# A hybrid decoder layer in split fp32: the high and low parts of its matmul operands placed 32 bytes apart modulo 512

## The chip, the cores and the metric

The kernel runs on one core of one Trainium2 chip. The metric is the device time of one execution in microseconds, the median over several runs. Durations of single instructions come from one profiled execution.

## The reference

One layer of a decoder, batch 1, 256 tokens, model width 2048, all float32. Cut to what matters:

```
proj = h @ w_in                      # 2048 x 6144: q, k, v of 8 differential and 8 MoBA heads of 128
a_out = diff_attention(q_d, k_d, v_d, lam, ...)   # two softmaxes a head, a norm over the head
b_out = moba_attention(q_m, k_m, v_m, ...)        # at 256 tokens: causal softmax attention
mix = concat(a_out, b_out) @ w_out   # 2048 x 2048
h = layer_norm(ALPHA * h + mix)
u = h @ w_up                         # 2048 x 11264: gate and value, 5632 columns each
f = (silu(causal_conv3(gate)) * value) @ w_down   # 5632 x 2048
out = layer_norm(ALPHA * h + f)
```

## The kernel before

**Split products.** Every large matmul is worked out in float32r with both operands cut in two: hi is the operand rounded (a ScalarE copy, lines 129, 799, 990, 1019), lo is the operand minus hi (a VectorE subtraction, lines 130, 809, 1003, 1023; for some, a ScalarE copy with the sign changed and an accumulating DMA from GpSimd's queue, lines 797 and 807). A product is the sum of hi by hi, hi by lo and lo by hi, all accumulated in one PSUM bank. The weights stream from HBM into raw tiles (four of 2048 columns), and from there into six tiles hl of 2 x 1024 columns, hi first and lo right behind it.

**Two forms of product.** In the feature form (`mm_feature`, line 206, for q and k, and `up_half`, line 829, for the up projection) the weights are the stationary operand and the activations stream. The activations lie as [hi of 256 tokens, lo of 256 tokens] for each block of 128 features, in the tiles x2 (xa, xb) and later h2 (ha, hb) in the same place. A block takes two matmuls: wh with all 512 columns, then wl with the 256 columns of hi. In the token form the activations are stationary and 512 columns of weights stream, three matmuls: (hi, wh), (hi, wl), (lo, wh). So work the v projection (stationary x2), the out projection (stationary mh and ml, `mm_token`, line 220, two banks at a time), the down projection (stationary aparts or pparts) and the tail (stationary tails). `mm_first` (line 561) does one block of the up projection in the token form with 256 columns.

Every matmul loads its own stationary operand; TensorE does this (PEld in the profile) beside the matmul before it.

**The down projection** is done in pairs of 128-feature blocks, by seven products instead of eight on sums and differences of activations and weights (`unit_weights`, `product`); the weight sums' parts are in bparts (in the place of z), one and hl. The last pairs of the second half are done plainly (`plain_weights`, `plain_product`), the last four blocks at the end (`split_tail`, `mm_tail`).

**Order.** The first stage (v, q, k, attention, out projection, first norm) is written out by hand, with attention's steps hung between weight tiles by `at`. From the third tile of the up projection on, a planner (`order`) simulates each engine with a cost for each task and sorts the tasks; groups of four down products are set between tiles of the up projection. Rings (`raw_ring`, `hl_ring`, `b_ring`, ...) tell it when buffers come free.

**Places in memory.** Tile pools are laid out one behind another in each partition, in the order in which they are opened: keep, raws, splits, small, then first and work in the first stage, zone and duo in their place afterwards. All large tiles are multiples of 512 bytes long. keep begins with the tile shift, of 32 bytes, which nothing uses; then come x2 (h2 later, tag t2), back (480 bytes) and z, so that x2 and h2 start 32 bytes above the other tiles, modulo 512, and z and all pools behind it start where they would without both. mh, ml and val are in first.

Of the kernel before, what the change touches and what calls it, by code (L numbers as in the profile page):

```python
# [16 lines left out]
P = 128  # L17
D = 2048
# [32 lines left out]
def hymba_layer(ctx: ExitStack, tc: tile.TileContext, a: dict):  # L51
# [18 lines left out]

    bank = [psum.tile([P, 512], F32, name=f"bank{i}") for i in range(8)]


    loaded, parts = {}, {}

# [39 lines left out]
    def split(i, half, both=None):  # L115

        if i >= NS or (i, half) in parts:
            return
        t = loaded[i] if half == 0 else loaded.pop(i)
        if both is None:  # L120
            both = splits.tile([P, 2, 1024], F32R, name="hl")
            hi, lo = both[:, 0], both[:, 1]
        else:
            hi, lo = both[:, half], both[:, 2 + half]
        for x, y in pieces(i, half):
            if i < 4 and x % 512 == 0:
                split_x(4 * i + x // 512, 4 * i + (y + 511) // 512)
            s = slice(x - 1024 * half, y - 1024 * half)
            ACT.activation(hi[:, s], t[:, x:y], AF.Copy)  # L129
            DVE.tensor_tensor(lo[:, s], t[:, x:y], hi[:, s].bitcast(F32), ALU.subtract)  # L130
        parts[i, half] = (hi, lo)
# [381 lines left out]
    for i in range(first_o, last[0]):  # L513
        begin(i)
        if i == last[0] - 1:
            both = first.tile([P, 4, 1024], F32R, name="both", tag="big")
# [268 lines left out]
    def split_up(n, x, by_dma):  # L785
# [1 line left out]
        deps = [load_task[n]] if n in load_task else []  # L787

        def alloc():
            both = splits.tile([P, 2, 1024], F32R, name="hl")  # L790
            hl_of[n, x] = both[:, 0], both[:, 1]

        def first():
            alloc()
# [135 lines left out]
    part_ring = Ring(2)  # L930
    part_of, part_use, part_done = {}, {}, {}

    def pair_parts(q, h):
        def high():
            t = part_of[q, h] = duo.tile([P, 2, 7 * P], F32R, name="aparts")
            ACT.activation(t[:, 0], acts[q].rearrange("p a b -> p (a b)"), AF.Copy)

        def low():
            t = part_of[q, h]
            DVE.tensor_tensor(t[:, 1], acts[q].rearrange("p a b -> p (a b)"), t[:, 0].bitcast(F32), ALU.subtract)  # L940
# [21 lines left out]
    def unit_weights(q, h):  # L962
# [24 lines left out]
        s_use += [t1, t2, t3, t4]  # L987

        def high_a():
            ACT.activation(U()["a"][:, 0], U()["raw"][:, 0:1024], AF.Copy)  # L990

        def new_a():
            U()["a"] = splits.tile([P, 2, 1024], F32R, name="hl")
            if apart:
                ACT.activation(U()["a"][:, 1], U()["raw"][:, 0:1024], AF.Copy, scale=-1.0)
            else:
                high_a()

        def low_a():
            if apart:  # L1000
                POOL.dma_start(U()["a"][:, 1], U()["raw"][:, 0:1024], accum_op=ALU.add)
            else:
                DVE.tensor_tensor(U()["a"][:, 1], U()["raw"][:, 0:1024], U()["a"][:, 0].bitcast(F32), ALU.subtract)

        def high_1():
            U()["1"] = zone.tile([P, 2, 512], F32R, name="one")
            ACT.activation(U()["1"][:, 0], raw("11"), AF.Copy)

        def low_1():
            DVE.tensor_tensor(U()["1"][:, 1], raw("11"), U()["1"][:, 0].bitcast(F32), ALU.subtract)  # L1010

        def high_b(j):
            if apart:
                t = splits.tile([P, 2, 1024], F32R, name="hl")
                U()["b", j] = t.rearrange("p j (c w) -> p j c w", c=2)
# [3 lines left out]
            ACT.activation(U()["b", j][:, 0], U()["T"][:, 2 * j:2 * j + 2], AF.Copy)  # L1019

        def low_b(j):
            b = U()["b", j]
            DVE.tensor_tensor(b[:, 1], U()["T"][:, 2 * j:2 * j + 2], b[:, 0].bitcast(F32), ALU.subtract)  # L1023

        ha = act(1024, new_a, [load])
        a_use = hl_ring.use(ha)
# [31 lines left out]
    def product(q, h, m, first, last):  # L1058
# [1 line left out]
        s = SLOT[left] * P  # L1060

        def fn():
            al = part_of[q, h][:, :, s:s + P]
            u = unit[q, h]
            if where == "a":
                wh, wl = (u["a"][:, j, 512 * c:512 * (c + 1)] for j in range(2))
            elif where == "1":
                wh, wl = u["1"][:, 0], u["1"][:, 1]
            else:
                wh, wl = (u["b", int(where[1])][:, j, c] for j in range(2))  # L1070
            dst = bank[m - 1]
            mm(dst, al[:, 0], wh, first, False)
            mm(dst, al[:, 0], wl, False, False)
            mm(dst, al[:, 1], wh, False, last)

        d = unit_done[q, h]
        deps = part_done[q, h] + d[where]
# [6 lines left out]
    def plain_parts(q):  # L1084
# [1 line left out]
            DVE.tensor_tensor(acts[q][:, 3], acts[q][:, 2], acts[q][:, 3], ALU.subtract)  # L1086

        def high():
            t = part_of[q, 1] = duo.tile([P, 2, 4 * P], F32R, name="pparts", tag="aparts")
            ACT.activation(t[:, 0], acts[q][:, 0:4].rearrange("p a b -> p (a b)"), AF.Copy)  # L1090

        def low():
            t = part_of[q, 1]
            DVE.tensor_tensor(t[:, 1], acts[q][:, 0:4].rearrange("p a b -> p (a b)"), t[:, 0].bitcast(F32), ALU.subtract)

        k = dve(P, back, act_use[q][2:])
        t0 = act(4 * P, high, [k])
# [6 lines left out]
    def plain_weights(q):  # L1104
# [3 lines left out]
        for j in range(2):  # L1108
            s = slice(1024 * j, 1024 * (j + 1))

            def high(j=j, s=s):
                U()[j] = splits.tile([P, 2, 1024], F32R, name="hl")
                ACT.activation(U()[j][:, 0], U()["raw"][:, s], AF.Copy)

            def low(j=j, s=s):
                DVE.tensor_tensor(U()[j][:, 1], U()["raw"][:, s], U()[j][:, 0].bitcast(F32), ALU.subtract)

            t = act(1024, high, [load])
            use = hl_ring.use(t)
# [6 lines left out]
    def plain_product(q, m):  # L1126
# [4 lines left out]
        stop = b == 7 and q == N_PAIRS - 1 and j == 1  # L1131

        def fn():
            al = part_of[q, 1][:, :, s:s + P]
            wh, wl = (unit[q, 1][j][:, x, 512 * c:512 * (c + 1)] for x in range(2))
            mm(bank[b], al[:, 0], wh, start, False)
            mm(bank[b], al[:, 0], wl, False, False)
            mm(bank[b], al[:, 1], wh, False, stop)
# [161 lines left out]
    def split_tail(i, x, by_dma):  # L1300
# [3 lines left out]
        def alloc():  # L1304
            if early:
                if i == 0:
                    tail_hl["first"] = keep.tile([P, 2, 2, 1024], F32R, name="first", tag="z")
                both = tail_hl["first"][:, i]
            else:
                both = splits.tile([P, 2, 1024], F32R, name="hl")  # L1310
            tail_hl[i, x] = both[:, 0], both[:, 1]

        def high(first):
            if first:
# [26 lines left out]

    def split_acts():
        def high(i):
            aps[i] = zone.tile([P, 2, S], F32R, name="tails", tag="act", bufs=9)
            ACT.activation(aps[i][:, 0], act_slot(2 * N_PAIRS + i).rearrange("p a b -> p (a b)"), AF.Copy)

        def low(i):
            src = act_slot(2 * N_PAIRS + i).rearrange("p a b -> p (a b)")
            DVE.tensor_tensor(aps[i][:, 1], src, aps[i][:, 0].bitcast(F32), ALU.subtract)

        for i in range(4):
            t = act(S, lambda i=i: high(i), [act_done[2 * N_PAIRS + i]])
# [8 lines left out]
    def mm_tail(dst, t, c, start, o=0, w=512):  # L1361
        ts = slice(t * P, (t + 1) * P)
        for i in range(4):
            x = c % 2 * 512 + o
            wh, wl = (y[:, x:x + w] for y in tail_hl[i, c // 2])
            ah, al = (aps[i][:, j, ts] for j in range(2))
# [204 lines left out]
```

## Time and profile before

| | |
|---|---|
| median of 3 runs | 1118.74 us (1117.76 to 1122.53) |
| the profiled execution | 1117.88 us, of which the span of instructions 1116.1 us |
| TensorE busy | 1100.2 us, 5878 matmuls |
| VectorE busy | 916.6 us |
| ScalarE busy | 702.3 us |
| GpSimd busy | 75.9 us |
| mean granted TensorE clock | 0.997 |
| DMA | 249.89 MB, 224 GB/s |

How to read the profile: PE is TensorE's matmuls and PEld its weight loads, DVE is VectorE, ACT ScalarE, POOL GpSimd, SP the queue that issues most DMAs. A group's line gives the code line, engine and operation, the tiles as output<-inputs, sizes, count, then busy time in us, the mean of one in ns, and the idle time before. All split matmuls have one line, 204 (the helper `mm`), so they are told apart by their tiles: bank<-moving,stationary. Matmuls are pipelined: the mean of one is longer than the time from the start of one to the start of the next.

### The profile page before, as it was taken

How to read it: one execution, taken by the hardware profiler on the slowest of the kernel's cores; microseconds unless marked ns; L12 is line 12 of the kernel's file. 1: busy time of each engine (PE TensorE's matmuls, PEld its weight loads, DVE VectorE, ACT ScalarE, POOL GpSimd, SP SyncE). 2: the span in 40 equal slices, each digit the busy share in tenths (PEclk: the TensorE clock that was granted, in tenths of full speed). 3: DMA queues.
4: the chain of work that ended last, by engine and by line, in shares of the span. 5: the costliest groups of instructions: out<-in, count | busy, mean ns of one | idle time of the engine just before them, and what ended most of it. 6: DMA issues, size and time to landing. Idle time of an engine off the chain costs nothing.

```text
span 1116.1 us, 15532 instructions
## 1 busy us (share of the span) xinstructions
PE 1100.2 (99%) x5878; PEld 944.9 (85%) x5878; DVE 916.6 (82%) x1485; ACT 702.3 (63%) x1022; POOL 75.9 (7%) x90
## 2 busy tenths in 40 slices
PE   9999999999999999999999999999999999999995
PEld 6888888888888898888888888888888888888884
DVE  6895886867855687789999768798999989898997
ACT  6565465444443386767767666766777676777671
POOL 0000000000000000000100100000100010001004
PEclk9999999999999999999999999999999999999998
DMA  9765445445455627777897978877877798769883
GB/s 333 293 226 194 156 159 180 168 172 177 163 188 188 226 104 278 231 263 256 262 251 243 243 209 264 260 238 225 228 253 230 229 247 252 234 220 272 248 263 127
DMA packets 48507, 249.89 MB, mean 224 GB/s; under 512 B 4784, under 2 KB 6704, under 8 KB 27824
## 3 DMA queue, kind: packets, MB, share of 16 engines
q1 hardware_dynamic: 39360, 221.11, 55.2%
q0 software_dynamic: 9072, 27.79, 13.8%
q8 instruction: 46, 0.75, 0.3%
q14 instruction: 29, 0.24, 0.1%
HBM read 216.90 MB, written 9.44 MB: 203 GB/s over the span
## 4 chain that ended last, share of the span: by engine, by line
PE 93%; DVE 4%; DMA 1%; ACT 1%; issue 0%; SPq 0%; POOL 0%; POOLq 0%; ACTq 0%; DVEq 0%
PE bank L204 93%; DMA raw<-in_w_v 1%; DVE st L393 1%; DVE z L390 1%; PE bank L327 0%; DVE z L1462 0%; DVE z L1373 0%; DVE hl L1327 0%; DVE spill L1386 0%; DVE bparts L1023 0%; PE bank L544 0%; SPq L152 0%; ACT bparts L1019 0%; DVE z L1458 0%; PE bank L374 0%
## 5 line engine op out<-in xcount | busy, mean ns | idle before, releaser
L204 PE MATMUL bank<-ha,hl 128*128 128x512 f32 x1376 | 253.9, 337 | 0.0
L204 PE MATMUL bank<-hb,hl 128*128 128x512 f32 x1376 | 252.7, 336 | 0.0
L204 PEld LDWEIGHTS bank<-ha,hl 128*128 128x128 f32 x1376 | 215.7, 188 | 30.9 <-ACT ev L903 0.4
L204 PEld LDWEIGHTS bank<-hb,hl 128*128 128x128 f32 x1376 | 211.7, 189 | 26.8
L130 DVE TENSOR_TENSOR hl<-raw,hl 128x1024 fp32r<-128x1024 f32 (+1 forms) x143 | 164.6, 1163 | 68.5 <-ACT hl L129 67.2
L129 ACT ACTIVATE hl<-raw 128x1024 fp32r<-128x1024 f32 (+1 forms) x143 | 143.7, 1009 | 91.7 <-PE bank L204 65.3
L809 DVE TENSOR_TENSOR hl<-raw,hl 128x1024 fp32r<-128x1024 f32 x128 | 154.9, 1221 | 19.7 <-ACT hl L799 19.2
L799 ACT ACTIVATE hl<-raw 128x1024 fp32r<-128x1024 f32 x128 | 133.1, 1053 | 35.4 <-PE bank L204 31.0
L204 PE MATMUL bank<-bparts,aparts 128*128 128x512 f32 x432 | 109.4, 391 | 0.8 <-DVE bparts L1023 0.8
L903 ACT ACTIVATE ev<-bank 128x512 f32<-128x512 f32 x86 | 51.3, 597 | 89.5 <-PE bank L204 89.5
L1023 DVE TENSOR_TENSOR bparts<-sums,bparts 128x1024 fp32r<-128x1024 f32 x72 | 85.9, 1222 | 18.6 <-ACT bparts L1019 18.6
L204 PE MATMUL bank<-xa,hl 128*128 128x512 f32 (+1 forms) x512 | 96.2, 341 | 0.0
L204 PE MATMUL bank<-xb,hl 128*128 128x512 f32 (+1 forms) x512 | 94.8, 338 | 0.0
L204 PEld LDWEIGHTS bank<-bparts,aparts 128*128 128x128 f32 x432 | 78.6, 188 | 17.4 <-DVE bparts L1023 1.7
L204 PEld LDWEIGHTS bank<-xa,hl 128*128 128x128 f32 x512 | 79.2, 189 | 11.9 <-issue 1.3
L204 PEld LDWEIGHTS bank<-xb,hl 128*128 128x128 f32 x512 | 78.7, 189 | 9.8
L1019 ACT ACTIVATE bparts<-sums 128x1024 fp32r<-128x1024 f32 x72 | 73.2, 1053 | 16.9 <-PE bank L204 7.8
L807 POOL DMA_DIRECT2D hl<-raw x39 | 34.1, 875 | 542.2 <-ACT hl L797 357.8
L204 PE MATMUL bank<-hl,mh 128*128 128x512 f32 x256 | 70.4, 392 | 0.0
L204 PE MATMUL bank<-hl,aparts 128*128 128x512 f32 x252 | 65.2, 390 | 0.0
L797 ACT ACTIVATE hl<-raw 128x1024 fp32r<-128x1024 f32 x39 | 41.1, 1055 | 26.1 <-PE bank L204 25.9
L204 PEld LDWEIGHTS bank<-hl,mh 128*128 128x128 f32 x256 | 47.7, 188 | 9.6
(167 smaller groups left out, 1428.3 us busy)
## 6 DMA issues: line engine op xcount, KB each, us to landing
raw<-in_w_u SPq DMA_DIRECT2D x88, 1024.0 KB, 6.0
raw<-in_w_d SPq DMA_DIRECT2D x42, 1024.0 KB, 7.1
raw<-in_w_qk SPq DMA_DIRECT2D x32, 1024.0 KB, 4.8
hl<-raw POOLq DMA_DIRECT2D x41, 512.0 KB, 5.5
raw<-in_w_o SPq DMA_DIRECT2D x16, 1024.0 KB, 4.8
raw<-in_w_v SPq DMA_DIRECT2D x12, 1024.0 KB, 4.8
zd<-spill POOLq DMA_DIRECT2D x20, 256.0 KB, 7.9
raw<-in_w_v SPq DMA_DIRECT2D x8, 256.0 KB, 4.8
```

Of the source, the lines that this page charges most:

```text
L129: ACT.activation(hi[:, s], t[:, x:y], AF.Copy)
L130: DVE.tensor_tensor(lo[:, s], t[:, x:y], hi[:, s].bitcast(F32), ALU.subtract)
L204: PE.matmul(out, lhsT, rhs, start=start, stop=stop)
L390: DVE.scalar_tensor_tensor(z[:, t, s], z[:, t, s], alpha, src, op0=ALU.mult, op1=ALU.add)
L393: DVE.bn_stats(stats[ln, t][:, c], z[:, t, s])
L797: ACT.activation(lo, raw_of[n][:, s], AF.Copy, scale=-1.0)
L799: ACT.activation(hi, raw_of[n][:, s], AF.Copy)
L807: POOL.dma_start(lo, raw_of[n][:, s], accum_op=ALU.add)
L809: DVE.tensor_tensor(lo, raw_of[n][:, s], hi.bitcast(F32), ALU.subtract)
L903: ACT.activation(evs[n], bank[b], AF.Copy)
L1019: ACT.activation(U()["b", j][:, 0], U()["T"][:, 2 * j:2 * j + 2], AF.Copy)
L1023: DVE.tensor_tensor(b[:, 1], U()["T"][:, 2 * j:2 * j + 2], b[:, 0].bitcast(F32), ALU.subtract)
```

## The change

Each tile that held hi and lo becomes either two tiles in two pools, or one tile 32 bytes longer in which lo lies first and hi after it with a gap of 32 bytes. shift is taken out. tiny (moved out of small, and 32 bytes shorter) lies between the pool of the hi tiles and the pool of the lo tiles. ml comes first in the pool first, then val, 32 bytes longer, then mh. In the down projection the activations' hi parts are in duo and their lo parts in zone. x2 and h2 keep hi and lo as they were. With that every lo lies 32 bytes below its hi, modulo 512 bytes. In `mm_token` the last two loops become one, so that with two banks the order of products is hi by wh0, hi by wh1, hi by wl0, lo by wh0, hi by wl1, lo by wh1. The core of the diff (the splits of weights and activations elsewhere follow the same pattern):

```diff
     keep = pool("keep")
-    shift = keep.tile([P, 8], F32, name="shift")
     raws = pool("raws", 4)
-    splits = pool("splits", 6)
+    his = pool("his", 6)
+    tiny = pool("tiny").tile([P, P - 8], F32, name="tiny")
+    los = pool("los", 6)
     small = pool("small")
-    tiny = small.tile([P, P], F32, name="tiny")
...
+    def two_parts():
+        return his.tile([P, 1024], F32R, name="hi"), los.tile([P, 1024], F32R, name="lo")
+
+    def low_first(t, w):
+        return t[:, w + 8:2 * w + 8], t[:, 0:w]
...
-            both = splits.tile([P, 2, 1024], F32R, name="hl")
-            hi, lo = both[:, 0], both[:, 1]
+            hi, lo = two_parts()
...
-    z = keep.tile([P, 2, D], F32, name="z", tag="z")
+    z = keep.tile([P, 2 * D + 8], F32, name="z", tag="z")[:, 0:2 * D].rearrange("p (t d) -> p t d", t=2)
...
         for c, d in enumerate(dst):
             mm(d, ah, w[c][1], False, False)
-        for c, d in enumerate(dst):
             mm(d, al, w[c][0], False, last)
...
-    mh = first.tile([P, NH, S], F32R, name="mh", tag="ma")
-    ml = first.tile([P, NH, S], F32R, name="ml", tag="mb")
+    ml = first.tile([P, NH, S], F32R, name="ml")
     vals = {}
-    val_all = first.tile([P, 3, 2, 512], F32, name="val", tag="big")
+    val_all = first.tile([P, 2 * D + 8], F32, name="val", tag="big")[:, 0:6 * 512].rearrange(
+        "p (g t c) -> p g t c", g=3, t=2)
+    mh = first.tile([P, NH, S], F32R, name="mh")
...
+    def new_parts():
+        return duo.tile([P, 7 * P], F32R, name="ahi"), zone.tile([P, 7 * P], F32R, name="alo", bufs=2)
...
-            U()["1"] = zone.tile([P, 2, 512], F32R, name="one")
-            ACT.activation(U()["1"][:, 0], raw("11"), AF.Copy)
+            U()["1"] = low_first(zone.tile([P, 1032], F32R, name="one"), 512)
+            ACT.activation(U()["1"][0], raw("11"), AF.Copy)
...
-                t = keep.tile([P, 2, 4, 512], F32R, name="bparts", tag="z")
-                U()["b", 0], U()["b", 1] = t[:, :, 0:2], t[:, :, 2:4]
+                t = low_first(keep.tile([P, 2 * D + 8], F32R, name="bparts", tag="z"), 2048)
+                U()["b", 0], U()["b", 1] = [y[:, 0:1024] for y in t], [y[:, 1024:2048] for y in t]
...
-            aps[i] = zone.tile([P, 2, S], F32R, name="tails", tag="act", bufs=9)
+            aps[i] = low_first(zone.tile([P, 2 * S + 8], F32R, name="tails", tag="act", bufs=9), S)
```

More of the change, by code (lines that the diff above doesn't have):

```diff
@@ L120, in split @@
         if both is None:
-            both = splits.tile([P, 2, 1024], F32R, name="hl")
-            hi, lo = both[:, 0], both[:, 1]
+            hi, lo = two_parts()
         else:
-            hi, lo = both[:, half], both[:, 2 + half]
+            hi, lo = (y[:, 1024 * half:1024 * half + 1024] for y in low_first(both, 2048))
         for x, y in pieces(i, half):
@@ L515, in hymba_layer @@
         if i == last[0] - 1:
-            both = first.tile([P, 4, 1024], F32R, name="both", tag="big")
+            both = first.tile([P, 2 * D + 8], F32R, name="both", tag="big")
             split(first_u + 1, 0, both)
@@ L789, in alloc @@
         def alloc():
-            both = splits.tile([P, 2, 1024], F32R, name="hl")
-            hl_of[n, x] = both[:, 0], both[:, 1]
+            hl_of[n, x] = two_parts()
         def first():
@@ L989, in high_a @@
         def high_a():
-            ACT.activation(U()["a"][:, 0], U()["raw"][:, 0:1024], AF.Copy)
+            ACT.activation(U()["a"][0], U()["raw"][:, 0:1024], AF.Copy)
         def new_a():
-            U()["a"] = splits.tile([P, 2, 1024], F32R, name="hl")
+            U()["a"] = two_parts()
             if apart:
-                ACT.activation(U()["a"][:, 1], U()["raw"][:, 0:1024], AF.Copy, scale=-1.0)
+                ACT.activation(U()["a"][1], U()["raw"][:, 0:1024], AF.Copy, scale=-1.0)
             else:
@@ L1062, in fn @@
         def fn():
-            al = part_of[q, h][:, :, s:s + P]
+            ah, al = (y[:, s:s + P] for y in part_of[q, h])
             u = unit[q, h]
[L1065 to L1070, printed above, removed]
+            w = u["b", int(where[1])] if where[0] == "b" else u[where]
+            wh, wl = (y[:, 512 * c:512 * (c + 1)] for y in w)
             dst = bank[m - 1]
-            mm(dst, al[:, 0], wh, first, False)
-            mm(dst, al[:, 0], wl, False, False)
-            mm(dst, al[:, 1], wh, False, last)
+            mm(dst, ah, wh, first, False)
+            mm(dst, ah, wl, False, False)
+            mm(dst, al, wh, False, last)
         d = unit_done[q, h]
@@ L1088, in high @@
         def high():
-            t = part_of[q, 1] = duo.tile([P, 2, 4 * P], F32R, name="pparts", tag="aparts")
-            ACT.activation(t[:, 0], acts[q][:, 0:4].rearrange("p a b -> p (a b)"), AF.Copy)
+            t = part_of[q, 1] = new_parts()
+            ACT.activation(t[0][:, 0:4 * P], acts[q][:, 0:4].rearrange("p a b -> p (a b)"), AF.Copy)
         def low():
             t = part_of[q, 1]
-            DVE.tensor_tensor(t[:, 1], acts[q][:, 0:4].rearrange("p a b -> p (a b)"), t[:, 0].bitcast(F32), ALU.subtract)
+            hi, lo = (y[:, 0:4 * P] for y in t)
+            DVE.tensor_tensor(lo, acts[q][:, 0:4].rearrange("p a b -> p (a b)"), hi.bitcast(F32), ALU.subtract)
         k = dve(P, back, act_use[q][2:])
@@ L1111, in high @@
             def high(j=j, s=s):
-                U()[j] = splits.tile([P, 2, 1024], F32R, name="hl")
-                ACT.activation(U()[j][:, 0], U()["raw"][:, s], AF.Copy)
+                U()[j] = two_parts()
+                ACT.activation(U()[j][0], U()["raw"][:, s], AF.Copy)
             def low(j=j, s=s):
-                DVE.tensor_tensor(U()[j][:, 1], U()["raw"][:, s], U()[j][:, 0].bitcast(F32), ALU.subtract)
+                DVE.tensor_tensor(U()[j][1], U()["raw"][:, s], U()[j][0].bitcast(F32), ALU.subtract)
             t = act(1024, high, [load])
@@ L1133, in fn @@
         def fn():
[L1134 to L1138, printed above, removed]
+            ah, al = (y[:, s:s + P] for y in part_of[q, 1])
+            wh, wl = (y[:, 512 * c:512 * (c + 1)] for y in unit[q, 1][j])
+            mm(bank[b], ah, wh, start, False)
+            mm(bank[b], ah, wl, False, False)
+            mm(bank[b], al, wh, False, stop)
         t = pe(0.7, fn, part_done[q, 1] + unit_done[q, 1][j] + (users(7) if start else []))
@@ L1306, in alloc @@
                 if i == 0:
-                    tail_hl["first"] = keep.tile([P, 2, 2, 1024], F32R, name="first", tag="z")
-                both = tail_hl["first"][:, i]
-            else:
-                both = splits.tile([P, 2, 1024], F32R, name="hl")
-            tail_hl[i, x] = both[:, 0], both[:, 1]
+                    tail_hl["first"] = low_first(keep.tile([P, 2 * D + 8], F32R, name="first", tag="z"), 2048)
+                tail_hl[i, x] = tuple(y[:, 1024 * i:1024 * i + 1024] for y in tail_hl["first"])
+            else:
+                tail_hl[i, x] = two_parts()
         def high(first):
@@ L1343, in high @@
         def high(i):
[L1344 to L1345 removed]
+            aps[i] = low_first(zone.tile([P, 2 * S + 8], F32R, name="tails", tag="act", bufs=9), S)
+            ACT.activation(aps[i][0], act_slot(2 * N_PAIRS + i).rearrange("p a b -> p (a b)"), AF.Copy)
         def low(i):
             src = act_slot(2 * N_PAIRS + i).rearrange("p a b -> p (a b)")
[L1349 removed]
+            DVE.tensor_tensor(aps[i][1], src, aps[i][0].bitcast(F32), ALU.subtract)
         for i in range(4):
@@ L1365, in mm_tail @@
             wh, wl = (y[:, x:x + w] for y in tail_hl[i, c // 2])
-            ah, al = (aps[i][:, j, ts] for j in range(2))
+            ah, al = (y[:, ts] for y in aps[i])
             mm(dst, ah, wh, start and i == 0, False)
```

24 lines of the change are left out of this document (13 added, 11 removed).

## The prediction

> **What bounds the kernel now.** I read the page first (share of each engine, idle time), then the chain of waits, then the matmul groups with different shapes kept apart, then short pieces of the timeline of the three kinds of matmul stream.
>
> ```profile
> span 1116.1 us, 15532 instructions
> PE 1100.2 (99%) x5878; PEld 944.9 (85%) x5878; DVE 916.6 (82%) x1485; ACT 702.3 (63%) x1022; POOL 75.9 (7%) x90
> PEclk9999999999999999999999999999999999999998
> PE 93%; DVE 4%; DMA 1%; ACT 1%; issue 0%; SPq 0%; POOL 0%; POOLq 0%; ACTq 0%; DVEq 0%
> ...
> L204 PE MATMUL bank<-ha,hl 128*128 128x512 f32 x688 | 243.5, 392 | 0.0
> L204 PE MATMUL bank<-hb,hl 128*128 128x512 f32 x688 | 242.3, 390 | 0.0
> L204 PE MATMUL bank<-hb,hl 128*128 128x256 f32 x688 | 194.2, 282 | 0.0
> L204 PE MATMUL bank<-ha,hl 128*128 128x256 f32 x688 | 194.1, 282 | 0.0
> L204 PE MATMUL bank<-bparts,aparts 128*128 128x512 f32 x432 | 109.4, 391 | 0.8 <-DVE bparts L1023 0.8
> L204 PE MATMUL bank<-xa,hl 128*128 128x512 f32 x256 | 92.4, 399 | 0.0
> L204 PE MATMUL bank<-xb,hl 128*128 128x512 f32 x256 | 90.9, 393 | 0.0
> L204 PE MATMUL bank<-hl,mh 128*128 128x512 f32 x256 | 70.4, 392 | 0.0
> L204 PE MATMUL bank<-hl,xa 128*128 128x512 f32 x192 | 48.1, 404 | 0.5 <-ACT hl L129 0.5
> L204 PE MATMUL bank<-hl,xb 128*128 128x512 f32 x192 | 47.5, 400 | 0.2 <-DVE hl L130 0.2
> L204 PE MATMUL bank<-hl,ml 128*128 128x512 f32 x128 | 40.8, 390 | 0.0
> L204 PE MATMUL bank<-hl,tails 128*128 128x512 f32 x60 | 14.3, 389 | 0.0
> L204 PE MATMUL bank<-hl,tails 128*128 128x256 f32 x24 | 3.0, 283 | 0.0
> ```
>
> TensorE is busy 99% of the span at an undisturbed clock (a row of nines), its matmuls are 93% of the chain that ended last, and they hardly wait: the idle column of the groups shows 0.8 us at most. So the time is the number of matmuls, which the change leaves alone, times the time from one matmul's start to the next, here called the step. The mean in these rows is not the step, since matmuls overlap; but a group with a longer step shows a longer mean. Among 512-column groups the means run from 389 to 404 for the same shape. The names read output, moving operand, stationary operand. The extremes differ in which pools the two operands come from, and that is what the change alters.
>
> ```profile
> 18.05 11.24 PE L204 MATMUL bank<-hl,xb 128*128 128x512 f32 x47 [0.22 <-DVE hl L130]
> 29.12 2.95 PE L204 MATMUL bank<-xa,hl 128*128 128x512 f32 x16
> ...
> 324.56 1.07 PE L204 MATMUL bank<-hl,mh 128*128 128x512 f32 x4
> 325.47 0.62 PE L204 MATMUL bank<-hl,ml 128*128 128x512 f32 x2
> ...
> 344.96 0.39 PE L204 MATMUL bank<-hl,mh 128*128 128x512 f32 x1
> ...
> 414.56 2.94 PE L204 MATMUL bank<-ha,hl 128*128 128x512 f32 x16
> ...
> 481.12 1.54 PE L204 MATMUL bank<-hl,aparts 128*128 128x512 f32 x6
> ```
>
> First column: start in us. The v projection has 47 matmuls from 18.05 to 29.12: 11.07/47 = 235.5 ns a step. The out projection goes 15 times through four mh and two ml matmuls, 90 in all, from 324.56 to 344.96: 226.7 ns. The up projection runs 24 groups of 16 (eight pairs of 512 and 256 columns) from 414.56 to 481.12: 66.56/192 = 346.7 ns a pair. So the same 512-column matmul is 8.8 ns dearer in the v projection than in the out projection.
>
> **The distances in memory.** Each matmul here loads its own stationary operand while the matmul before it streams its moving operand. I take as the quantity that matters the distance, modulo 512 bytes, from the operand being loaded to the one being streamed at that time; it is an inference from the rows above. All large tiles are multiples of 512 bytes, so the distances come from the small ones. Before, the 32-byte tile shift puts x2 and h2 32 bytes above all other parts. Hence: features (q, k, up: x2 or h2 streams, hl is loaded) +32 for both matmuls of a pair; v (hl streams, x2 is loaded) -32 for all; out and down projections 0 for all.
>
> After: shift is gone, so x2, h2, his and mh stand at the base, and los, ml, alo 32 below (tiny, of 480 bytes, stands between his and los; val is 32 bytes longer between ml and mh; the tiles of zone add up to 59,936 bytes = 117 x 512 + 32, so that duo, with ahi, is at the base again). In the pair, the 512 columns of wh's matmul stream while wl is loaded: +32 as before; the 256 columns of wl's stream while the next wh is loaded: 0, was +32. In v, the order wh, wl, wh streams while ah, al, next ah is loaded: 0, -32, 0, was -32 three times. In the out projection the new order streams wh0, wh1, wl0, wh0, wl1, wh1 while ah, ah, al, ah, al, next ah is loaded: hi against hi and lo against lo, 0 everywhere as before (the old order would have given -32 and +32 once each in six). Down projection and tail: 0 as before.
>
> **The change part by part.** No matmul, split or DMA is added or removed.
>
> *v projection.* 192 + 192 matmuls. At most all of 384 x 8.8 ns = 3.4 us goes. Two of three get the distance of the out projection, so 2.3 us if each is priced by itself, 0 (or a little worse than 0) if the mix never settles. Later pieces are nearer the good step than the first:
>
> ```profile
> 86.71 5.87 PE L204 MATMUL bank<-hl,xa 128*128 128x512 f32 x24
> 92.42 0.38 PE L374 MATMUL bank<-ident,on 128*128 128x128 f32 x2
> ```
>
> 5.71 us for 24 is 238 ns, with one slow start after attention's small matmuls in it; taking about 0.1 us off for that leaves 233, 6 ns too much. I take 384 x 2/3 x 6 ns = **-1.5 us**.
>
> *Features, 512 columns.* Distance +32 before and after: 0 by itself. What can change is their neighbour, below.
>
> *Features, 256 columns.* 688 + 688 + 256 + 256 = 1,888 pairs, 60% of the time. Distance 0 with 256 columns is seen in the tail: mean 283, against 282 in the up projection: +1 ns x 1,888 = +1.9 us. The other end: 512 columns have 389 to 391 at distance 0 and 390 to 399 at +32, so 0 may be the cheaper one, as far as -1.9 us. The row of the same shape is nearer; a mean is rounded, so I take half: **+1.0 us**.
>
> *Change of stage.* ha follows the down products and hb follows ha; ha's mean is 392, hb's 390, and bparts has 391 against 390 of the others: 688 x 2 + 432 x 1 ns = 1.8 us is what changing between +32 and 0 costs now at most. The last matmul of a pair now has the products' own distance, which halves the change: between 0 and -1.8, I take **-0.5 us**.
>
> ```profile
> 704.87 1.54 PE L204 MATMUL bank<-bparts,aparts 128*128 128x512 f32 x6
> 706.24 1.52 PE L204 MATMUL bank<-hl,aparts 128*128 128x512 f32 x6
> 707.60 2.96 PE L204 MATMUL bank<-ha,hl 128*128 128x512 f32 x16
> 710.39 1.78 PE L204 MATMUL bank<-hb,hl 128*128 128x512 f32 x9
> ```
>
> Here it is in the timeline: 1.37 us for the first six products and 1.36 for the next six, and 2.79 us for eight pairs after the products where 66.56/24 = 2.77 is usual.
>
> *Out projection's order.* Successive matmuls now go to the same bank twice; a run of the v projection and the products do so already, the latter at 706.24 with 1.36/6 = 226.7 ns. **0.**
>
> *Hi and lo in two tiles.* The low part on VectorE (or its accumulating DMA on GpSimd's queue) can now have to wait by itself until matmuls are through with the old lo, where ScalarE's write of the shared tile had waited for both. Behind it on VectorE stand the next sums and low parts, and TensorE waits for those. The cover is VectorE's idle time:
>
> ```profile
> 800.00:900.00 100.00, 100.00 (x533) 86.48 (x532) 90.85 (x128) 70.55 (x88) 5.23 (x6) 1.00 0.79 246
> L809 DVE TENSOR_TENSOR hl<-raw,hl 128x1024 fp32r<-128x1024 f32 x128 | 154.9, 1221 | 19.7 <-ACT hl L799 19.2
> ```
>
> Columns 2 to 5 of the first row are TensorE, weight loads, VectorE and ScalarE: in the fullest stretch of the steady part VectorE has 9 us of 100 to spare. An added wait would have to cost over 9.15 us in some 128 instructions, 71 ns each, before TensorE feels it. A low part's own duration (1,221 ns) may move either way with the write 32 bytes off its reads; 7% more on all of them would use up the same cover. **0.** The release of hi before lo is finished can only make ScalarE earlier, and it isn't waited for.
>
> *Start and end of the program* keep their chain: **0**.
>
> **Sum.** -1.5 + 1.0 - 0.5 = -1.0 us. The profiled execution took 1117.88 us, of which the span is 1116.1; so 1116.9 for it. The median of the runs shown, 1118.74, is 0.9 above the profiled one: I predict 1117.7. The three runs lie between 1117.76 and 1122.53, so that I call anything within 0.5%, or 5.6 us, no change.
>
> **A rule weighed.** The 235.5 and 226.7 ns above are for equal shapes. The Trainium skill, SBUF — State Buffer, section "Who interferes with whom", says that TensorE's two reads, of the moving and of the stationary operand, have ports of their own and never wait for anyone; by that rule addresses cannot matter, and the sum would be 0: 1118.7. The trace disagrees as far as 8.8 ns a matmul go. The same skill, TensorE: Matmul & The Clock Gate, section "Back-to-back issue gap", gives N/2.4 + 2.5 ns, or 215.7 ns for 512 columns; no run here shows that for these matmuls, and 11 ns below the best row on every feature matmul would be an estimate of 42 us to win, from that page.
>
> **Rivals.**
> *The pair does not settle (slower).* The step after a change of stage shows that a stream needs several matmuls to come back to its good value. Now the distance alternates +32, 0 within each pair, so it could be at the bad value always. Its place is the 512-column matmul of each pair. At the full price of the v projection: 1,888 x 8.8 = 16.6 us, with 1.9 for the 256 columns, +18 us: 1137. At half: 8.3 + 1.9 - 0.5 = +9.7: 1128.4. It decides from 3 ns a pair (5.6 us/1,888). For it: v's run of 47 stays bad although each matmul has the same distance, so not every pattern settles. Against: the 256-column means, 282 and 283, do not care about distance.
> *Every stream falls to its best row (faster).* 512 columns in features from 392, 390, 399 and 393 to 389: 688 x 3 + 688 x 1 + 256 x 10 + 256 x 4 = 6.3 us, some of it slow starts; v's 3.4 us with it: -9.7: 1109. For it: distance 0 has the lowest means everywhere. Against: features keep +32 in the matmul concerned.
> *The fixed part of the step goes (faster).* 512 and 256 columns differ by 390 - 282 = 108 ns, so of the 226.7 some 226.7 - 216 = 11 ns do not scale with the columns. If these too are a clash between loading and streaming, and 0 after +32 avoids it on half of the feature matmuls: 1,888 x 11 = 21 us: 1098. Against: no group shows it anywhere, at any distance.
> *Addresses play no part.* Then v's step comes from elsewhere (its first run is also the stretch where weights arrive at the highest rate), and the time is 1118.7; within the forecast's own range.
>
> **How the numbers follow.** Forecast, with addresses playing no part: 0.50; own range 1113.5 to 1122. Pair that does not settle, beyond 3 ns: 0.25. Best row everywhere: 0.18. Fixed part: 0.07. So faster 0.25, same 0.50, slower 0.25. For 8 in 10 the range takes in the best row (1109) with a little beyond it, and the unsettled pair to somewhat above its half price: 1106 to 1130; left out are the fixed part and the unsettled pair at full price.
>
> **What would show it.** v: means of hl,xa and hl,xb at 396 or below, a run of 47 in 10.7 to 10.9 us instead of 11.07. Features: eight pairs in 2.77 to 2.79 us; 2.81 or more means the unsettled pair, 2.75 or less a gain that I do not expect. Out projection: 15 rounds in 20.4 us. VectorE: L809 between 1.2 and 1.25 us, no idle time of TensorE put down to it. The prediction is wrong if the up projection's pair leaves 345 to 349 ns: with 1,888 of them, everything else is small beside it.

## The result and the profile after

The changed kernel takes 1131.43 us (median of 6 runs, 1130.94 to 1132.86), the kernel before beside it 1118.85 (1117.76 to 1122.53). The ratio is 1.0109, 95% interval 1.0093 to 1.0126: slower by 12.6 us, where 1117.7 was forecast.

The page of the kernel after, its span, engines, granted clock and shares of the chain that ended last:

```profile
span 1129.7 us, 15565 instructions
PE 1114.2 (99%) x5878; PEld 943.9 (84%) x5878; DVE 916.7 (81%) x1485; ACT 702.9 (62%) x1022; POOL 75.9 (7%) x90
PEclk9999999999999999999999999999999999999998
PE 93%; DMA 2%; DVE 2%; issue 2%; ACT 1%; SPq 0%; POOL 0%; ACTq 0%; POOLq 0%
```

The matmuls are the same 5878, the clock is the same, VectorE is as busy as before to 0.1 us and ScalarE to 0.6; TensorE's busy time has grown by 14.0 us, and the span of the profiled execution by 13.6. So TensorE does not wait longer: the matmuls themselves follow each other more slowly. The groups by shape (busy us, mean ns of one; idle time before):

```profile
L209 PE MATMUL bank<-hb,hi 128*128 128x512 f32 x688 | 246.9, 395 | 0.0
L209 PE MATMUL bank<-ha,hi 128*128 128x512 f32 x688 | 245.8, 394 | 0.0
L209 PE MATMUL bank<-hb,lo 128*128 128x256 f32 x688 | 193.7, 282 | 0.0
L209 PE MATMUL bank<-bparts,ahi 128*128 128x512 f32 x288 | 90.5, 394 | 0.8 <-DVE bparts L1031 0.8
L209 PE MATMUL bank<-lo,mh 128*128 128x512 f32 x128 | 50.4, 394 | 0.0
L209 PE MATMUL bank<-hi,xa 128*128 128x512 f32 x128 | 42.6, 401 | 1.1 <-ACT hi L134 1.1
L209 PE MATMUL bank<-lo,xa 128*128 128x512 f32 x64 | 25.6, 400 | 0.2 <-DVE lo L135 0.2
```

The 512-column means have risen from 390-392 to 393-396 in the up and down projections, and to 394-398 in the out projection; v (moving hi or lo, stationary xa) has fallen from 404 to 400-401. The chain of waits in order of time (start, length, what) gives the price without overlap, since in it a stream of matmuls without a wait is one line. x322 is nearly the out projection, x400 is the up projection alone (200 pairs), x3061 the up and down projections mixed. Before, then after:

```profile
318.57 72.80 PE bank L204 x322
411.95 69.35 PE bank L204 x400
484.18 571.85 PE bank L204 x3061
```

```profile
321.32 74.43 PE bank L209 x322
416.42 70.68 PE bank L209 x400
489.98 580.00 PE bank L209 x3061
```

A pair went from 346.7 ns to 353.4. The timeline of after, in the up projection:

```profile
560.00 0.39 PE L209 MATMUL bank<-hb,hi 128*128 128x512 f32 x1
560.23 0.28 PE L209 MATMUL bank<-hb,lo 128*128 128x256 f32 x1
560.35 0.40 PE L209 MATMUL bank<-hb,hi 128*128 128x512 f32 x1
560.59 0.28 PE L209 MATMUL bank<-hb,lo 128*128 128x256 f32 x1
560.71 0.39 PE L209 MATMUL bank<-hb,hi 128*128 128x512 f32 x1
```

Two pairs take 0.71 us, where two settled ones take 0.69. That each matmul has a row of its own here only means that hi and lo are two tiles now; before, with the one tile hl, the view drew 16 in one row. Starts subtracted in ns (up projection, near 440 us) show the difference: before, the steps repeat as 228, 119, 228, 118, after as 235, 124, 231, 116. In the out projection (near 330 us) they were 226 to 227 throughout and are 224 to 236 now. Below, a stream at the lowest steady step that was seen for its shape (226.7 ns for 512 columns, 346.7 for a pair) is called settled, one above it unsettled.

Summed over the whole trace (each matmul's start subtracted from the next one's, in us; attention, the transposes and the 96 matmuls of `mm_first` are left out), here with the experiments that are told below:

| kernel | v | q, k | out | up | down and tail |
|---|---|---|---|---|---|
| before | 92.6 | 180.7 | 87.8 | 478.4 | 216.0 |
| after | 91.9 | 183.5 | 89.6 | 485.2 | 219.5 |
| k1_apart | 92.2 | 180.7 | 87.8 | 478.4 | 216.0 |
| k3_noshift | 91.1 | 183.7 | 87.8 | 484.2 | 216.8 |
| ka_weights | 92.3 | 183.5 | 89.5 | 485.8 | 219.3 |
| s16 | 92.6 | 181.2 | 87.8 | 478.0 | 218.0 |
| lo_above | 91.7 | 180.7 | 89.6 | 477.7 | 220.1 |
| base0 | 90.6 | 183.7 | 87.8 | 484.2 | 216.8 |
| mixed | 90.5 | 180.7 | 87.8 | 478.0 | 216.9 |

After minus before: -0.7, +2.8, +1.8, +6.8, +3.5, together +14.2 us; the loss is in every stage that had been settled. In before and k1_apart all operands lie at the same places; they differ by 0.4 us in v, where waits for the first weights are counted too, and by nothing in the other columns. The subtraction for the weights' low parts on VectorE (after, groups by line) has the duration it had:

```profile
L813 DVE TENSOR_TENSOR lo<-raw,hi 128x1024 fp32r<-128x1024 f32 x128 | 154.9, 1221 | 19.7 <-ACT hi L803 18.5
```

### The profile page after: what moved, and what is told of

It is laid out like the page before. It is cut to its first block, busy times and chain, and to the rows that moved or that the text cites. A ratio compares the mean times of both kernels' runs of the same rounds, so it can differ in the third digit from the quotient of the medians.

```text
span 1129.7 us, 15565 instructions
## 1 busy us (share of the span) xinstructions
PE 1114.2 (99%) x5878; PEld 943.9 (84%) x5878; DVE 916.7 (81%) x1485; ACT 702.9 (62%) x1022; POOL 75.9 (7%) x90
## 4 chain that ended last, share of the span: by engine, by line
PE 93%; DMA 2%; DVE 2%; issue 2%; ACT 1%; SPq 0%; POOL 0%; ACTq 0%; POOLq 0%
PE bank L209 92%; DMA raw<-in_w_v 1%; DMA rawt<-in_w_d 1%; PE bank L332 0%; DVE z L1467 0%; DVE st L398 0%; DVE z L395 0%; DVE bparts L1031 0%; PE bank L549 0%; SPq L157 0%; ACT bparts L1027 0%; DVE z L1463 0%; PE bank L379 0%; SPq L118 0%; POOL rstd L406 0%
## 5 line engine op out<-in xcount | busy, mean ns | idle before, releaser
L209 PE MATMUL bank<-hb,hi 128*128 128x512 f32 x688 | 246.9, 395 | 0.0
L209 PE MATMUL bank<-ha,hi 128*128 128x512 f32 x688 | 245.8, 394 | 0.0
L135 DVE TENSOR_TENSOR lo<-raw,hi 128x1024 fp32r<-128x1024 f32 (+1 forms) x143 | 164.7, 1163 | 68.4 <-ACT hi L134 67.4
L134 ACT ACTIVATE hi<-raw 128x1024 fp32r<-128x1024 f32 (+1 forms) x143 | 143.7, 1009 | 91.1 <-PE bank L209 64.6
L209 PE MATMUL bank<-hb,lo 128*128 128x256 f32 x688 | 193.7, 282 | 0.0
L209 PE MATMUL bank<-ha,lo 128*128 128x256 f32 x688 | 193.4, 281 | 0.0
L813 DVE TENSOR_TENSOR lo<-raw,hi 128x1024 fp32r<-128x1024 f32 x128 | 154.9, 1221 | 19.7 <-ACT hi L803 18.5
L209 PEld LDWEIGHTS bank<-hb,hi 128*128 128x128 f32 x688 | 129.3, 188 | 31.6
L209 PEld LDWEIGHTS bank<-ha,hi 128*128 128x128 f32 x688 | 129.2, 188 | 31.1 <-ACT ev L907 0.4
L803 ACT ACTIVATE hi<-raw 128x1024 fp32r<-128x1024 f32 x128 | 133.1, 1053 | 30.5 <-PE bank L209 29.3
L209 PE MATMUL bank<-bparts,ahi 128*128 128x512 f32 x288 | 90.5, 394 | 0.8 <-DVE bparts L1031 0.8
```

Source lines behind the costliest of these rows:

```text
L209: PE.matmul(out, lhsT, rhs, start=start, stop=stop)
L803: ACT.activation(hi, raw_of[n][:, s], AF.Copy)
L813: DVE.tensor_tensor(lo, raw_of[n][:, s], hi.bitcast(F32), ALU.subtract)
```

## The experiments

The letters in the expectations: A is that a stream in which the distance alternates does not settle; B that another distance counts than the one I took; D that two pools, or the new order of the out projection, are dear whatever the addresses; F that a map of good and bad places decides, and not constancy (for features, lo above hi settles, lo below does not); G that what streamed earlier decides. C and E are explained where they occur. Kernels m1 to m4 leave the layer out and measure streams of matmuls alone.

**m1_offsets: which streams settle.** For each pattern 120 float32r matmuls, each with its own weight load; a row is named by its pattern (columns of successive matmuls, byte offsets of the moving operand, of the stationary one).

```diff
+PATTERNS = {
+    "c0x": ([512], [0], [0]),
...
+    "c32x": ([512], [32], [0]),
...
+    "tripa": ([512], [32, 0, 32], [32, 32, 0]),
...
+    "paftx": ([512, 256], [32], [32, 0]),
+    "prevx": ([512, 256], [0], [0, 32]),
...
+            PE.matmul(bank[0][:, 0:w], s[:, y:y + P], m[:, x:x + w], start=True, stop=True)
```

> Leaves the layer out: 34 streams of 120 float32r matmuls each on the same data, with nothing else running, that differ only in where their operands lie modulo 512 bytes. Names: c = 512 columns at one constant distance (moving minus stationary, in bytes), p = pairs of 512 and 256 columns at a constant distance, q = 256 columns, alts = the loaded operand alternates by 32 bytes, altm = the streamed one does, next = both do, so that what streams and what is loaded meanwhile stay at the same place, own = both do, so that each matmul's own two operands are at the same place, tripa = the token form of the changed kernel, paft = its feature form. Theory A (alternation: a stream settles only where loads keep their place among themselves and streams keep theirs): c0 and p0 step like the settled streams of before, 227 ns and 347 a pair; alts, altm, next, own, tripa 231 to 233 on average, paft 352 a pair. Rival B (the distance between what streams and what is loaded meanwhile, as in the prediction): next and tripa 227, since their distance is always 0, alts and altm dearer. Rival C (addresses play no part): all streams of one shape within 1 ns.

The timeline, start and length of a pattern's 120 matmuls (of a few):

```profile
7.50 27.59 PE L104 MATMUL bank<-mc0x,sc0x 128*128 128x512 f32 x120
62.73 28.17 PE L104 MATMUL bank<-mc32x,sc32x 128*128 128x512 f32 x120
230.22 27.38 PE L104 MATMUL bank<-mc256x,sc256x 128*128 128x512 f32 x120
451.22 27.76 PE L104 MATMUL bank<-mnextx,snextx 128*128 128x512 f32 x120
506.62 27.96 PE L104 MATMUL bank<-mtripa,stripa 128*128 128x512 f32 x120
724.11 21.35 PE L104 MATMUL bank<-mpaftx,spaftx 128*128 128x512 f32 x120
745.30 20.97 PE L104 MATMUL bank<-mprevx,sprevx 128*128 128x512 f32 x120
```

The steady step, taken over whole repeats in the second half of each stream, is for 512 columns 226.7 ns at a constant distance of 0, 256 and -16 bytes, 228.9 at 64 and 320, 231.6 to 233.3 at 16, 32, 48, 96, 128, 192, 384, 448 and 480. No other engine works in that half (ScalarE writes the next pattern's tiles in the first 2.1 us of a stream), so the differences need no other engine. Three patterns settle the dispute over distance. "next" and "tripa" have distance 0 from each operand loaded to the one streaming meanwhile, as I counted it, and do not settle (230.0 and 231.7); so my zero is not enough once the places themselves alternate. "paft" is the changed kernel's pair: 353.4 ns a pair, against 346.7 for the old pair (p32), with the same repeat of 235, 124, 231, 116 ns as in the layer. But "prev", with lo 32 bytes above hi, alternates as well and settles at 346.6; so A in its plain form falls too. And p0, with no offset at all, gives 353.3. (The expectations give pairs as 173.9 and 177.3 ns a matmul. Halves of the true pairs are 173.3 and 176.7; a mean that counts one 512-column step more than 256-column ones is up to 0.6 higher.)

**k1_apart: the change without the 32 bytes.** Two pools and the new order stay; hi and lo come back to one place modulo 512, x2 and h2 32 above.

```diff
+    shift = keep.tile([P, 8], F32, name="shift")
-    tiny = pool("tiny").tile([P, P - 8], F32, name="tiny")
+    tiny = pool("tiny").tile([P, P], F32, name="tiny")
-        return t[:, w + 8:2 * w + 8], t[:, 0:w]
+        return t[:, w:2 * w], t[:, 0:w]
...
```

> The changed kernel with its tiles and pools apart and its order of products, but all 32-byte gaps taken out and x2 and h2 raised by 32 bytes again: every operand lies modulo 512 where it lay before. Theory A and rival B (addresses): 1118 to 1120 us, up projection 2.77 us for eight pairs, products 226.7 ns. Rival D (the cost comes from two tiles in two pools: finer waits, other release, the new order): 1130 to 1132.

1118.95 us, ratio 1.0000 (0.9990 to 1.0009). In the chain in order of time:

```profile
318.23 72.80 PE bank L210 x322
411.61 69.35 PE bank L210 x400
483.85 571.86 PE bank L210 x3061
```

The three lengths of before to 0.01 us. D falls; the whole loss comes with the 32 bytes.

**k3_noshift: before, without the tile shift** (all large tiles at one place modulo 512).

```diff
-    shift = keep.tile([P, 8], F32, name="shift")
-    back = keep.tile([P, P - 8], F32, name="back")
+    back = keep.tile([P, P], F32, name="back")
```

> The kernel before with x2 and h2 32 bytes lower, so that all operands lie at the same place modulo 512 (distance 0 everywhere). Theory A: everything is constant, so all streams settle, v too: up projection 346.7 ns a pair, v 227 ns, no price for the change of stage; 1114 to 1117 us. Rival B as the prediction had it: v gains 2 to 3 us, the pair is unknown between 346.7 and 352: 1116 to 1126. Rival E (the constant distance itself decides, and features need 32): the pair rises to 350 or more, 1125 or more.

1126.33, ratio 1.0068 (1.0053 to 1.0083). The chain in order of time:

```profile
413.87 69.35 PE bank L203 x400
486.10 578.30 PE bank L203 x3061
```

v gains 1.5 us and features lose 8.8; A's 1114 to 1117 is a miss. The up projection alone, which follows a few small matmuls, is settled at distance 0 (69.35), and loses it once down products are mixed in (578.30 against 571.85): of the 62 streams of pairs that follow down products 61 end at 353.3 ns a pair. So the distance alone does not decide, and what streamed before is the likely cause.

**ka_weights: only the weights' lo lowered**, of the activations only lo in zone.

```diff
+    pool("pad").tile([P, 8], F32, name="pad")
+    mh = first.tile([P, NH, S], F32R, name="mh")
-    mh = first.tile([P, NH, S], F32R, name="mh")
...
-            aps[i] = low_first(zone.tile([P, 2 * S + 8], F32R, name="tails", tag="act", bufs=9), S)
+            aps[i] = (lambda t: (t[:, S:2 * S], t[:, 0:S]))(zone.tile([P, 2 * S], F32R, name="tails", tag="act", bufs=9))
```

> The changed kernel with only the weights' lo 32 bytes lower (but the small tile one); mh and ml, the activations' parts of the down projection and the tail's at the same place modulo 512. Theory A: in features the loads still alternate, in v, out and down projection the streams still alternate: as the changed kernel, 1130 to 1133. Rival B: out and down projection now have distances 0, -32, 0 instead of 0, so they are dearer than in the changed kernel by up to 3 us or the same: 1131 to 1135. Rival D: 1130 to 1132.

1132.42, ratio 1.0120 (1.0104 to 1.0135): the weights' share alone costs as much as the whole change, in out (89.5) and down (219.3) too. A, B and D all allow this time, so that it does not choose among them. Lowering the activations' lo with them bought nothing.

**m2_offsets: a map of the pair.** m1's kernel with 25 pairs of constant distances. In a name the first part is the distance while wl is loaded, the second while the next wh is loaded; n is minus, p plus. The changed kernel is p32p0.

> Leaves the layer out again: 34 streams of 120 float32r matmuls. f = pairs of 512 and 256 columns; the two numbers (n below, p above zero) are the distances of what streams from what is loaded meanwhile, first during the 512 columns, then during the 256. t = the token form with hi above lo by that many bytes (n: lo above hi). c = one constant distance. Theory A (only what alternates is dear): the equal distances fp16p16, fp32p32 and tp256 if the period is 256 bytes step at N columns plus 13.3 ns, everything unequal at 16 or 17 ns. Rival F (a map of good and bad places, not of constancy, as prev against paft in the first such run suggests): fn32p0 good, fp32p0 bad, fp0p0 bad, and other unequal ones good too.

```profile
50.10 20.97 PE L104 MATMUL bank<-mfn32p0x,sfn32p0x 128*128 128x512 f32 x120
467.77 21.35 PE L104 MATMUL bank<-mfp32p0x,sfp32p0x 128*128 128x512 f32 x120
509.76 20.96 PE L104 MATMUL bank<-mfp32p32x,sfp32p32x 128*128 128x512 f32 x120
530.57 28.02 PE L104 MATMUL bank<-mtn32x,stn32x 128*128 128x512 f32 x120
```

Of the 25 pairs 17 settle at 173.3 ns a matmul, four lie at 174.4 to 175.7, four at 176.6 to 176.7, the changed kernel's among them; its mirror image n32p0 settles. Each ran once, behind one other stream; m4 shows that this can matter. The token form's three products do not settle for lo 32 above (tn32, 232.2) any more than for lo 32 below; they do for lo 256 above (226.7). Chains of 512 columns at 8, -8 and -24 bytes have 233.3 ns.

**s16: x2 and h2 16 bytes up instead of 32**, since m2 has the pair at +16 settled and m1 has chains at -16 settled.

```diff
-    shift = keep.tile([P, 8], F32, name="shift")
...
+            t = keep.tile([P, 2 * D + 8], F32R, name=f"{name}{j}", tag=f"t2{j}")
+            out.append(t[:, 4:2 * D + 4].rearrange("p (k j t) -> p k j t", k=KT // 2, j=2))
```

> The kernel before with x2 and h2 16 bytes above the other operands where they were 32; else the same layout. Theory F: features at distance +16 settle as at +32 (346.7 ns a pair), v at -16 settles at 226.7 ns instead of 234; 2 us less: 1115 to 1118. Rival B of the prediction (distance 0 is the good one and the price grows with it): v half its excess, 1117 to 1119. Rival E: features need just 32: over 1124.

1120.84, ratio 1.0016 (1.0007 to 1.0025): a miss. Features are as settled as expected (478.0), but v stays at 92.6, and down rises to 218.0. So the chain that settled alone at -16 did not foretell v. The two differ in more than what ran before: in m1 the stationary operand lay at a multiple of 32 bytes and the moving one 16 off it, in s16 the other way round. Which of these counts is not shown.

**lo_above: the change turned over**, lo 32 above hi.

```diff
-        return t[:, w + 8:2 * w + 8], t[:, 0:w]
+        return t[:, 0:w], t[:, w + 8:2 * w + 8]
...
```

> The changed kernel turned round: every lo 32 bytes above its hi, modulo 512, all else the same. Theory A (alternation by itself): as the changed kernel, 1130 to 1133. Theory F: features (distance -32 with the 512 columns, 0 with the 256) settle at about 347 ns a pair, v, out and down projection do not: 10 us of the changed kernel's 12.6 go back, 1121 to 1125.

1121.71, ratio 1.0021 (1.0012 to 1.0030), 9.7 us under the changed kernel's median by the sign of 32 bytes. The chain in order of time:

```profile
318.11 74.37 PE bank L210 x322
413.13 69.36 PE bank L210 x400
```

F holds: pairs settled (69.36, after 70.68), out projection as unsettled as after (74.37 against 74.43). Its timeline:

```profile
477.81 0.40 PE L210 MATMUL bank<-ha,hi 128*128 128x512 f32 x1
478.04 0.28 PE L210 MATMUL bank<-ha,lo 128*128 128x256 f32 x1
478.16 0.39 PE L210 MATMUL bank<-ha,hi 128*128 128x512 f32 x1
478.39 0.28 PE L210 MATMUL bank<-ha,lo 128*128 128x256 f32 x1
478.50 0.40 PE L210 MATMUL bank<-ha,hi 128*128 128x512 f32 x1
```

Single rows again, but 0.69 us for two pairs where after has 0.71.

**m3_bases: is it the place itself?** Pairs and chains at distance 0 at 16 places, 16 bytes apart.

> Leaves the layer out: 35 streams of 120 float32r matmuls. p = pairs of 512 and 256 columns at distance 0, c = 512 columns at distance 0; the number is the place of both operands modulo 256 bytes. again = p128 a second time, zero = p0 a second time, plus = place 128 with the streamed operand 32 bytes higher. Theory F with the place itself counting (p at 160 settled in the first run for 32 alone, the pair at distance 0 did not settle at 160 and did at 0): p0 173.9 ns a matmul, p128 and p160 177.3, c at most places 226.7, again as p128 and zero as p0. Rival G (the state left by the stream before decides, not the place): again or zero unlike its first run.

```profile
7.96 21.15 PE L105 MATMUL bank<-mp0x,sp0x 128*128 128x512 f32 x120
49.85 21.36 PE L105 MATMUL bank<-mp32x,sp32x 128*128 128x512 f32 x120
216.68 20.97 PE L105 MATMUL bank<-mp160x,sp160x 128*128 128x512 f32 x120
```

Pairs settle at 173.3 at 14 places, p16 has 174.2 and p32 176.7. p128 and p160 settle, against F with the place itself counting; "again" and "zero" end like their first runs (173.3), so that G's sign does not show here either. One thing speaks for a stream's history: the place called p160 is the one at which m1's p0 was unsettled, behind another stream (and in the other of the two buffers that the tiles take in turn). Chains are a miss: at the eight places that are multiples of 32 bytes they settle (226.7), at the eight that lie 16 above one they stay at 230.0 ns:

```profile
341.50 27.41 PE L105 MATMUL bank<-mc0x,sc0x 128*128 128x512 f32 x120
368.74 27.77 PE L105 MATMUL bank<-mc16x,sc16x 128*128 128x512 f32 x120
```

The two buffers change from stream to stream just as these places do, so the run cannot tell which of the two it is.

**base0: before, with every tile at place 0 modulo 256.**

```diff
-    shift = keep.tile([P, 8], F32, name="shift")
+    shift = keep.tile([P, 32], F32, name="shift")
-    back = keep.tile([P, P - 8], F32, name="back")
```

> The kernel before without the 32 bytes and with all large tiles 128 bytes further up, so that every operand lies at 0 modulo 256 (they lay at 128, x2 and h2 at 160). Theory F with the place itself counting: features, v, out and down projection all settle and nothing is paid at a change of stage: 4 us less, 1114 to 1117. Theory that the distance alone counts: as the run without the 32 bytes, 1126. Rival G: between.

1126.89, ratio 1.0064 (1.0050 to 1.0078), a miss, and the same as k3_noshift stage by stage to 0.1 us, but for v (0.5): whether all lies at 128 or at 0 modulo 256 plays no part. Only these two places were tried in the layer.

**m4_starts: what went before.** Each pattern behind 24 matmuls of 512 columns (a, b, c: distance 0, 32, 96) or of 256 (d, e: 0, 32); 96 matmuls each.

> Leaves the layer out: 30 streams of 96 float32r matmuls, six patterns (both32 = feature pair as before, below = feature pair of the changed kernel, above = lo 32 above hi, none = distance 0, chain = 512 columns at distance 0, triple = token form of the changed kernel), each after five other streams of 24 matmuls (a to e). Theory F (places alone): each pattern has one step whatever went ahead: both32, above, chain at N columns plus 13.3 ns, below and triple 16.5 to 18.5. Rival G (a stream keeps the state it falls into): some patterns, none above all, have two steps, 173.9 and 177.3 ns, by what went ahead; below and triple always the dear one.

```profile
13.88 16.80 PE L111 MATMUL bank<-mboth32a,sboth32a 128*128 128x512 f32 x96
36.00 17.12 PE L111 MATMUL bank<-mbelowa,sbelowa 128*128 128x512 f32 x96
58.41 16.80 PE L111 MATMUL bank<-mabovea,sabovea 128*128 128x512 f32 x96
80.50 16.81 PE L111 MATMUL bank<-mnonea,snonea 128*128 128x512 f32 x96
...
463.53 17.11 PE L111 MATMUL bank<-mbelowd,sbelowd 128*128 128x512 f32 x96
502.87 17.11 PE L111 MATMUL bank<-mnoned,snoned 128*128 128x512 f32 x96
```

Before's pair (both32) and lo above settle after every start, the changed kernel's pair (below) after none: 0.31 us over 48 pairs, 6.5 ns a pair, as in the up projection. The pair at distance 0 (none) has two states, settled after a, b, c (346.7 ns) and not after d, e (353.3). So one and the same pair at distance 0 can be good or dear, as in k3_noshift and base0. What puts it into the dear state there is not shown: the down products ahead of it in the layer are 512-column matmuls at distance 0 like start a, after which it settles here.

**mixed: the settled choice for each stage** (all at one place, lo 32 above hi for the features' weights alone).

```diff
-    shift = keep.tile([P, 8], F32, name="shift")
+    def two_parts(feature):
+        t = splits.tile([P, 2048 + 64], F32R, name="hl")
+        o = 1032 if feature else 1024
+        return t[:, 0:1024], t[:, o:o + 1024]
...
```

> The kernel before with x2 and h2 at the same place as all else, and lo 32 bytes above hi (modulo 256) in the weight tiles of the features alone; the weights of v, out and down projection have no gap. Theory F and G: features settle as with lo above (0.3 us over the settled step in all), v settles as without the 32 bytes (0.6 us over it, 2.5 before), out projection as before, down projection 1 to 2 us over it for the changes of stage: 1 to 3 us less than before, 1116 to 1118. Rival (a price for the longer tiles, or features settle only where the whole kernel has the gap): 1119 or more.

1117.78, ratio 0.9994 (0.9985 to 1.0002): not told from before, though within the 1116 to 1118 expected. In the table v gains 2.1 us, features keep what they had, down gives 0.9 back. No version here is clearly faster than before.

## Why the prediction was wrong

*Features.* This is the step that failed most: +9.6 us (q, k 2.8, up 6.8) where 0 for the 512 columns and +1.0 for the 256 stood. I priced the pair's two matmuls each by the distance it has by itself, and took the price of the 256 columns from a mean in the groups. That mean is 282 before and after; the pair costs 6.65 ns more all the same ((70.68 - 69.35)/200), because a mean is the length of one matmul and not the step. In lo_above the 512-column mean is as high as after's, 394, and yet the pair is settled. The pair settles or not as a whole: m1's "paft" and m4's "below" show it with only TensorE at work, lo_above and k1_apart in the layer. The prediction named the right place to look: the pair left its 345 to 349 ns.

*Out and down projections.* They stood at 0, "distance 0 everywhere as before", and cost +1.8 and +3.5. The distance was counted rightly; what is wrong is that it decides. Patterns "next" and "tripa" have it at 0 and are unsettled, because the places alternate. The second step that failed, and no rival had it.

*v.* -1.5 predicted, -0.7 measured, of which k1_apart has 0.4 with no place changed; the means are 398 to 401, not 396 or below. x2 keeps its hi and lo at one place, so only the weights alternate here. The stream 0, -32, 0 has no price per matmul by distance: v's undisturbed steps average 232.2 ns where they were 233.4, near the 231.7 of m1's "tripa" and far from the 226.7 of a settled stream. (5.61 us for 24 is 233.8 ns, so the forecast's own sum would have been -1.8.) What v could gain is seen with one place for all: 90.5 in mixed, -2.1.

*Change of stage*, -0.5: not separable from the pair, so neither shown nor refuted. *Out projection's order*, 0: right, 72.80 us in k1_apart with the new order. *Two tiles*, 0: right, the row of L813 has 1221 ns as L809 had, and k1_apart has the two pools at no cost. *Start and end*: the span grew by 0.6 us less than the stages of the table, so nothing was added there.

*The rivals.* "The pair does not settle" was the right mechanism in its place, and past its point of decision (3 ns a pair; 6.65 in the undisturbed stretch). It named 1137 at full price and 1128.4 at half; the measured 9.6 us is near its half price of 9.7, but that is luck: its terms were half of 8.8 ns, 1.9 us for the 256 columns by themselves and -0.5, where the pairs cost 5.1 ns each on average. The rest, 5.3 us, comes from out and down. Its against, that 256-column means do not care, was the misreading above. "Best row everywhere" and "the fixed part goes" fall: in some 130 streams of the four small kernels the lowest steady step is 226.7 ns for 512 columns and 346.7 for a pair, the values that before had already. A chain of 256 columns has 120.0 at distance 0, so that by these 256 columns are worth 106.7 ns and 13.3 are fixed. At a distance of 32 it has 117.8, and 116.7 in m4's start streams; no place took anything off the 512 columns or the pair. "Addresses play no part" falls with k1_apart against after, 12.5 us with the same instructions.

*The rule weighed.* By the Trainium skill, SBUF — State Buffer, "Who interferes with whom", as the prediction read it, addresses could not matter. The measurements decide against that for these matmuls: 226.7 against 233.3 ns in m1, with only TensorE at work in the steps that are counted. The other rule, of the Trainium skill's TensorE: Matmul & The Clock Gate, "Back-to-back issue gap", gives N/2.4 + 2.5 ns for a single isolated matmul, 215.8 ns for 512 columns. No float32r stream reached it; the bfloat16 matmuls of 512 columns with which each small kernel begins, each with its own weight load, did (215.8 ns over the last six steps). So no place won any of the 11 ns that lie between that rule and the best float32r step.

What stays open is why a pattern locks: the runs show which repeat of places settles, not the mechanism in the hardware. Open too is which history makes the pair at distance 0 dear in the layer, and whether a chain's place modulo 32 bytes counts. For a mix of stages (s16, down in mixed) small streams did not foretell the layer.

## What to carry to other kernels

When TensorE is busy 99% without a wait, subtract starts over whole repeats of a pattern before reading means: a pair here lost 1.9% behind means that differ by 1% or not at all. How the timeline merges rows goes by tile names and says nothing of the steps. Where operands are placed relative to each other can be worth 1% of such a kernel, so a change of pool sizes or order, made for any other reason, should keep places modulo 256 bytes or be timed. Price a repeating stream as a whole, measured in the order in which the kernel runs it, not matmul by matmul.

## What the runs showed of the hardware

- Distances count modulo 256 bytes, not 512: 0 and 256 are alike (226.7 ns), 64 and 320 (228.9), 16 and 272 (231.6 and 231.7), 128 and 384 nearly (233.3 and 232.2), and the triple at 256 apart settles (226.7) where those at 16, 32 and 64 apart have 231.7 to 233.3.
- The sign counts: with the moving operand at the place of hi, lo 32 bytes above hi gives 346.7 ns a pair, 32 below 353.3, after every one of m4's five starts.
- Some streams have two states and keep the one they fall into for as long as they last: the pair at distance 0 has 346.7 or 353.3 ns in m4 to the end of its 96 matmuls, by the 24 matmuls ahead of it.
